# The first half's output projection as seven products, and attention chunks loaded from ScalarE's queue

## The chip, the cores and the metric

The kernel runs on one core of a Trainium2 chip. The metric is the time of one execution on the device, in microseconds (us). The time before is a median of three runs. One further execution was profiled, and all views of the profile come from that one.

## The reference

One layer of a hybrid decoder block, on 2048 tokens of width 1024, in float32. The cut to what matters here:

```python
h = rmsnorm(x, norm1_g)
q, k, v, g, a, c_b, c_c, c_h = split(h @ w_in)            # gate a: rank 16
log_a = log_sigmoid(a @ w_gate_up + b_gate) / 16
o = gla_chunked(q / 8, k, v, log_a)                       # 4 heads, 64 x 128; state runs over the tokens
o_gla = rmsnorm(o, gla_norm_g) * silu(g)                  # width 512
o_conv = c_b * causal_depthwise_conv(c_c * c_h, conv_w)   # width 512, 3 taps
x = x + concat([o_gla, o_conv]) @ w_out                   # the output projection, 1024 x 1024
h2 = rmsnorm(x, norm2_g)
x = x + (silu(h2 @ w_ffn_gate) * (h2 @ w_ffn_up)) @ w_ffn_down
return rmsnorm(x, norm_f_g)
```

## The kernel before, in words

The 2048 tokens are four blocks (b) of 512, two to a half. All work is written in one function, and a scheduler of the framework, which simulates the engines, places each instruction; the order on every engine is then fixed in the program, and semaphores order the engines among one another.

**Products in float32.** Each operand is split into a high and a low part: ScalarE rounds (L146), VectorE subtracts (L147). A step of a product is then three matmuls, 128 x 128 by 128 x 512, lines L328 to L330: high by high, high by low, low by high.

**Two forms of a projection.** `unit` multiplies a 2 x 2 arrangement of quarters, two blocks of output columns by the two token blocks of a half, in seven products instead of eight (Strassen's scheme): seven products of four steps of three matmuls, 84 in all. It takes sums of weight quarters, which `unit_weights` makes on the way (seven splits, four combinations on GpSimd at L311 to L318), and operands in seven forms: the token operand's quarters B11, B21, B22 and the combinations T1 to T4. After a product `copied` takes a bank to SBUF on ScalarE (L348), and `plus` adds a bank on VectorE (L352). The plain form, in `out_proj`, needs eight products and only the operand's quarters: a half's output projection is 384 matmuls (L722, L723, L725) with 16 operand pairs, which `build_mix` loads as split values, from `s_gla` (attention) and `s_mix` (convolution).

**The sequence.** `in_proj(0)`, `in_proj(1)` (12 units each), `out_proj(0)`, `out_proj(1)`, then the feed-forward part in two halves. `in_proj(1)` begins with 28 operand pairs loaded from `s_h1` (`siB`, `siT` in the profile), which were made beside `in_proj(0)`. The operand pool holds 28 pairs, so loads of a next stage wait for products of the last.

**Attention in the background.** `gla_half` is a generator that treats a half's eight chunks of 128 tokens: `gla_load` (14 transfers of 64 KB on SyncE's queue, then the decay factors, L609 to L612), `gla_scores` (L617 to L638), `gla_outputs` (L641 to about L690) and `gla_finish` (transposes L682, gating L683, a split and two stores to `s_gla`). `tick`, called after each product, advances the background on every second product, and a second generator list, `ahead`, on every fourth. The gate's decays are made by another background generator, `gate`, during in_proj. Buffers of attention come from the pool `bx` (11, tag "b"), most others from `tp` (9, tag "t").

`in_proj` stores q, k, v and g of each block to scratch in DRAM (`s_kq`, `s_v`, `s_g`; the gate's `s_d`), one tile to 128 rows, and at its end the convolution's values, split, to `s_mix`.

Of the kernel before, what the change touches and what calls it, by code (L numbers as in the profile page):

```python
# [47 lines left out]
def tile_hymba_block(ctx, tc, x, xt, win, wa, wgu, wout, wffn, wdown, wdown_first, small, out):  # L48
# [50 lines left out]
            [dram.tile([P, PB], F32, name=f"{name}{b}_{i}") for i in range(n)] for b in range(NB)  # L99
        ]  # L100

    s_kq, s_d, s_v, s_g = scratch("sk", 4), scratch("sd", 2), scratch("sv", 4), scratch("sg", 4)
    s_x1 = scratch("sx", KD)
    s_mix = [[dram.tile([P, 2, PB], F32, name=f"sm{b}_{k}") for k in range(4)] for b in range(NB)]
    s_gla = [dram.tile([P, HEADS, 2, PB], F32, name=f"sgla{b}") for b in range(NB)]
    s_act = [
        [
# [17 lines left out]
    def col(c):  # L125
        return sml[:, c : c + 1]
# [13 lines left out]
    def store(dst, src):  # L140
        return nc.sync.dma_start(dst, src)
# [32 lines left out]


    background = []
    pace, ahead, hurry = [0], [], []

    def step():
        while background:  # L180
# [6 lines left out]
    def tick():  # L187
        pace[0] += 1
        if pace[0] % 2 == 0 or hurry:
            step()  # L190
        elif ahead and pace[0] % 4 == 1:
            next(ahead[0], None)

    def unhurried():
# [95 lines left out]
        return ops, [(r, j, o[r, j], True) for j in range(2) for r in range(2)]  # L290

    def weight_quarter(src):
        n = src.shape[-1]
        h = wqp.tile([P, 2, PB], F32R, name="wq", tag="wq")[:, :, 0:n]
        split(src, h[:, 0, :], h[:, 1, :])
        return h

    def raw_weights(src):
# [3 lines left out]
        raw_loads.append(load(raw, src))  # L302
        return raw

    def unit_weights(src):
        raw = raw_weights(src)
        n = src.shape[-1]
        a11, a12, a22, a21 = [raw[:, i, :] for i in range(4)]
        s1 = rawp.tile([P, PB], F32, name="s1", tag="s1", bufs=1)[:, 0:n]
        w = {"A11": weight_quarter(a11)}  # L310
        pool.tensor_tensor(s1, a21, a22, ALU.add)  # L311
        pool.tensor_tensor(a21, a11, a21, ALU.subtract)  # L312
        pool.tensor_tensor(a11, s1, a11, ALU.subtract)  # L313
# [4 lines left out]
        pool.tensor_tensor(a12, a12, a11, ALU.subtract)  # L318
        w["S4"] = weight_quarter(a12)
        w["A22"] = weight_quarter(a22)  # L320
        return w
# [7 lines left out]
        pe.matmul(o[:], wh, xl, start=False, stop=False, skip_group_check=True)  # L329
        return pe.matmul(o[:], wl, xh, start=False, stop=k == n - 1, skip_group_check=True)  # L330

    def unit(src, ops, into=None):


        w = unit_weights(src)
# [171 lines left out]
    def forget_gate(b, a_sb):  # L507
# [3 lines left out]
        for i in range(2):  # L511
# [20 lines left out]
            store(s_d[b][i][:], t2[:])  # L532
            yield
        decays[b] = em, dn, el

    def in_proj(half, ops, first):
# [7 lines left out]
        units = units()  # L544
        for dst, i0 in ((s_kq, 0), (s_kq, 2), (s_v, 0), (s_v, 2)):
            for r, j, c, p in next(units):
                store(dst[2 * half + j][i0 + r][:], settled(c, p)[:])
        for i0 in (0, 2):
            for r, j, c, p in next(units):
                store(s_g[2 * half + j][i0 + r][:], silu(c, p)[:])  # L550
        background.append(gla_half(half))
        for i0 in (0, 2):
            cc = {(r, j): settled(c, p) for r, j, c, p in next(units)}
# [14 lines left out]
            for r, j, c, _ in next(units):  # L568
                y = cc[r, j]
                dve.tensor_tensor(y[:], c[:], y[:], ALU.mult)  # L570
                hi = tp.tile([P, PB], F32R, name="hi", tag="t")
                split(y[:], hi[:], y[:].bitcast(F32R))
                dst = s_mix[2 * half + j][i0 + r]
                store(dst[:, 0, :], hi[:].bitcast(F32))
                store(dst[:, 1, :], y[:])


    def gla_half(half):
        chunks = [(b, t) for b in (2 * half, 2 * half + 1) for t in range(PT)]
        with tc.issue_after(last_silu[0].ins):  # L580
            tables = act.preload_act_table_set("natural_log_exp_and_others")
        with tc.issue_after(tables.ins):
            nxt = gla_load(*chunks[0])
        o = None
        for n, (b, t) in enumerate(chunks):
            cur = nxt
            s = gla_scores(b, t, *cur)
            yield
            if o is not None:
                gla_finish(*chunks[n - 1], *o)  # L590
                yield
            if n + 1 < len(chunks):
                nxt = gla_load(*chunks[n + 1])
            o = gla_outputs(b, t, *s)
            yield
        gla_finish(b, t, *o)
        done.add((b, t))
        yield
# [4 lines left out]
    def gla_load(b, t):  # L603
        s = slice(t * P, (t + 1) * P)
        kq, e, vt, g = [bt(n, (P, 4, P)) for n in ("kq", "ee", "vt", "gt")]
        for dst, src in ((kq, s_kq[b]), (e[:, 2:4, :], s_d[b]), (vt, s_v[b]), (g, s_g[b])):
            for i, r in enumerate(src):
                load(dst[:, i, :], r[:, s])
        act.activation(e[:, 0:2, :], e[:, 2:4, :], AF.Exp, scale=-1.0 / 16.0)  # L609
# [5 lines left out]
        return kq, e, vt, g  # L615
# [62 lines left out]
    def gla_finish(b, t, osb, g):  # L678

        ot = ps.tile([P, HEADS, P], F32, name="ot", tag="mm")  # L680
        for h in range(HEADS):
            pe.transpose(ot[:, h, :], osb[:, h, :], ident[:])  # L682
# [418 lines left out]
```

## Time and profile before

| what | value |
|---|---|
| time, median of 3 runs | 2146.97 us (2140.72 to 2151.3) |
| profiled execution: its time, its span | 2146.09 us, 2144.2 us |
| TensorE busy, share of span | 2043.6 us, 95% |
| VectorE, ScalarE, GpSimd busy | 68%, 47%, 46% |
| moved by DMA | 467.64 MB, mean 218 GB/s |
| in_proj(1), about 315 to 628 us: TensorE busy | 306.20 of 313 us |
| out_proj(0), about 628 to 727 us: TensorE busy | 98.65 of 99 us |

In the views a matmul group has the line, the engine, the tile names (out<-in), the shape and the count, and after the bar the busy time and the mean of one in ns, then the idle time in front of it and what released it. TensorE's matmuls overlap, so that the mean of one is not the distance between two. In the views by window a row has the stretch and its length, the busy time of PE (TensorE matmuls), PEld (its weight loads), DVE (VectorE), ACT (ScalarE) and POOL (GpSimd) with the number of instructions, then TensorE's granted clock, the DMA engines' share and their rate. SP is SyncE, which issues DMAs. A timeline row begins with the start and the duration in us, and ends with the idle time before it in brackets.

### The profile page before, as it was taken

To read this page: it belongs to the slowest core of one execution; us is meant where nothing else is said; L and a number is where in the kernel's file an instruction comes from. 1 tells how busy PE (TensorE), PEld (TensorE's weight loads), DVE (VectorE), ACT (ScalarE), POOL (GpSimd) and SP (SyncE) were. 2 spreads that over 40 slices of the span, in tenths; PEclk is the share of its full clock that TensorE was granted. 3 is DMA by queue.
4 is the path that set the end of the run, shared out by engine and by line. 5 is a ranking of instruction groups with operands and counts; after the bars stand their busy time and mean duration, and the time that the engine had idled before them with its cause. 6 is when DMAs were issued, how large, how long until landed. Compare 5 with 4: busy or idle time off the path is not lost.

```text
span 2144.2 us, 26906 instructions
## 1 busy us (share of the span) xinstructions
PE 2043.6 (95%) x9133; PEld 1651.3 (77%) x9133; DVE 1452.5 (68%) x2034; ACT 1012.1 (47%) x1962; POOL 997.0 (46%) x714
## 2 busy tenths in 40 slices
PE   4899899999999999999999999999999999999996
PEld 2677687887888887788888887787888888887775
DVE  8849965556774486888887664554686677664554
ACT  4555434574544235555454553333454454553344
POOL 4526422122201274655655436774644654445774
PEclk9999999999999999999999999999999999999998
DMA  4259658532577884465464577689455455487662
GB/s 150 76 199 315 218 228 286 156 125 79 166 247 256 309 294 152 167 240 220 172 237 182 185 303 283 254 336 355 157 191 205 154 197 196 172 329 293 266 265 108
DMA packets 189977, 467.64 MB, mean 218 GB/s; under 512 B 19856, under 2 KB 65168, under 8 KB 180112
## 3 DMA queue, kind: packets, MB, share of 16 engines
q1 hardware_dynamic: 189840, 465.93, 59.9%
q8 instruction: 72, 1.18, 0.2%
q14 instruction: 65, 0.53, 0.1%
HBM read 297.03 MB, written 168.82 MB: 217 GB/s over the span
## 4 chain that ended last, share of the span: by engine, by line
PE 70%; DVE 11%; DMA 8%; issue 4%; ACT 3%; POOL 3%; SPq 1%; DVEq 0%; POOLq 0%; ACTq 0%
PE mm L328 20%; PE mm L330 20%; PE mm L329 19%; DVE wq L147 3%; PE mm L722 3%; PE mm L725 3%; PE mm L723 3%; DMA raw<-in_wdown_dram 2%; DVE h L440 2%; DMA raw<-in_wffn_dram 1%; DVE so L147 1%; DVE op L147 1%; DMA op<-shT 1%; DVE c L352 1%; ACT wq L146 1%
## 5 line engine op out<-in xcount | busy, mean ns | idle before, releaser
L328 PE MATMUL mm<-op,wq 128*128 128x512 f32 x2495 | 982.1, 395 | 33.0 <-ACT c L348 20.3
L330 PE MATMUL mm<-op,wq 128*128 128x512 f32 x2495 | 967.6, 392 | 12.4 <-DVE wq L147 11.2
L329 PE MATMUL mm<-op,wq 128*128 128x512 f32 x2495 | 975.6, 391 | 2.5 <-DVE op L147 2.5
L147 DVE TENSOR_TENSOR wq<-raw,wq 128x512 fp32r<-128x512 f32 (+2 forms) x628 | 536.6, 860 | 320.2 <-ACT wq L146 318.3
L146 ACT ACTIVATE wq<-raw 128x512 fp32r<-128x512 f32 (+2 forms) x628 | 367.1, 589 | 566.7 <-PE mm L330 415.4
L328 PEld LDWEIGHTS mm<-op,wq 128*128 128x128 f32 x2495 | 470.4, 189 | 152.1 <-ACT c L348 27.1
L330 PEld LDWEIGHTS mm<-op,wq 128*128 128x128 f32 x2495 | 470.5, 189 | 121.9 <-DVE wq L147 22.4
L329 PEld LDWEIGHTS mm<-op,wq 128*128 128x128 f32 x2495 | 470.7, 189 | 99.8 <-DVE op L147 3.0
L313 POOL TENSOR_TENSOR raw<-s,raw 128x512 f32<-128x512 f32 (+2 forms) x98 | 130.7, 1333 | 437.7 <-DVE wq L147 403.1
L352 DVE TENSOR_TENSOR c<-mm,c 128x512 f32<-128x512 f32 x270 | 185.1, 686 | 100.1 <-PE mm L330 98.0
L311 POOL TENSOR_TENSOR s<-raw 128x512 f32<-128x512 f32 (+2 forms) x98 | 130.8, 1335 | 207.9 <-DMA raw<-in_wffn_dram 96.1
L318 POOL TENSOR_TENSOR raw<-raw 128x512 f32<-128x512 f32 (+2 forms) x98 | 130.4, 1331 | 129.5 <-DVE wq L147 128.9
L348 ACT ACTIVATE c<-mm 128x512 f32<-128x512 f32 x270 | 156.4, 585 | 23.8 <-PE mm L330 23.0
L704 POOL TENSOR_TENSOR ssx<-ssx,q 128x512 f32<-128x512 f32 x52 | 75.2, 1459 | 151.0 <-ACT q L703 151.0
L312 POOL TENSOR_TENSOR raw<-raw 128x512 f32<-128x512 f32 (+2 forms) x98 | 137.2, 1400 | 4.6
L884 POOL TENSOR_TENSOR y<-c,y 128x512 f32<-128x512 f32 x66 | 98.6, 1496 | 67.3 <-DVE c L352 67.2
L147 DVE TENSOR_TENSOR so<-t,so 128x512 fp32r<-128x512 f32 x100 | 89.6, 902 | 23.8 <-ACT so L146 23.6
L722 PE MATMUL mm<-op,wq 128*128 128x512 f32 x256 | 100.9, 394 | 0.0
L723 PE MATMUL mm<-op,wq 128*128 128x512 f32 x256 | 99.7, 390 | 0.0
L146 ACT ACTIVATE wq<-s 128x512 fp32r<-128x512 f32 (+2 forms) x98 | 57.6, 588 | 89.2 <-PE mm L330 86.6
L147 DVE TENSOR_TENSOR wq<-s,wq 128x512 fp32r<-128x512 f32 (+2 forms) x98 | 81.9, 835 | 15.6 <-ACT wq L146 15.2
L146 ACT ACTIVATE so<-t 128x512 fp32r<-128x512 f32 x100 | 62.9, 630 | 48.6 <-DMA sa_B<-so 19.9
(177 smaller groups left out, 1931.2 us busy)
## 6 DMA issues: line engine op xcount, KB each, us to landing
raw<-in_wffn_dram SPq DMA_DIRECT2D x44, 1024.0 KB, 6.1
sa_T<-so SPq DMA_DIRECT2D x88, 512.0 KB, 4.9
op<-sa_T SPq DMA_DIRECT2D x88, 512.0 KB, 9.6
sa_B<-so SPq DMA_DIRECT2D x69, 512.0 KB, 3.4
op<-sa_B SPq DMA_DIRECT2D x69, 512.0 KB, 9.2
raw<-in_win_dram SPq DMA_DIRECT2D x24, 1024.0 KB, 5.7
raw<-in_wdown_dram SPq DMA_DIRECT2D x24, 768.0 KB, 6.1
sx<-y SPq DMA_DIRECT2D x48, 256.0 KB, 3.4
```

What stands on the lines that cost most here:

```text
L146: last_hi[:] = [act.activation(hi, src, AF.Copy)]
L147: return dve.tensor_tensor(lo, src, hi.bitcast(F32), ALU.subtract)
L311: pool.tensor_tensor(s1, a21, a22, ALU.add)
L312: pool.tensor_tensor(a21, a11, a21, ALU.subtract)
L313: pool.tensor_tensor(a11, s1, a11, ALU.subtract)
L328: pe.matmul(o[:], wh, xh, start=first and k == 0, stop=False, skip_group_check=True)
L329: pe.matmul(o[:], wh, xl, start=False, stop=False, skip_group_check=True)
L330: return pe.matmul(o[:], wl, xh, start=False, stop=k == n - 1, skip_group_check=True)
L348: act.activation(t[:], o[:], AF.Copy)
L352: dve.tensor_tensor(t[:], o[:], t[:], ALU.add)
L722: pe.matmul(o[e, j][:], wh, m[:, 0, :], start=k == 0, stop=False)
L723: pe.matmul(o[e, j][:], wh, m[:, 1, :], start=False, stop=False)
```

## The change

- The scratch tiles `s_kq`, `s_d`, `s_v`, `s_g` become one tile to a block. `gla_load` is now four transfers (`ee` 128 KB, `kq`, `vt`, `gt` 256 KB each) issued by ScalarE instead of 14 issued by SyncE, and in `gla_half` it stands ahead of `gla_finish` instead of behind it. The decays move to a function of their own, `gla_decay`, called after `gla_outputs`. `done` is now told of every chunk, and not only of a half's last one.
- For the first half, the attention's and the convolution's values are stored unsplit, to `s_val`. A generator `mix_ahead`, in the list `ahead`, loads them during in_proj(1), makes the seven forms of operands (16 subtractions on GpSimd, 28 splits) and stores them to `s_mixp`. B21, B22 and B11 come as their values are there; T1 to T4 in twelve steps after chunk (1,3), the last of the first half. With the list `often` filled, `ahead` advances on every odd product.
- `out_first` takes the place of `out_proj(0)`: four calls of `unit` with `mixed=True` (which rearranges the output weights' layout in SBUF to quarters), that is 4 x 84 = 336 matmuls, with 28 operand pairs loaded from `s_mixp`. `out_proj(1)` stays as it is.

```diff
-    s_kq, s_d, s_v, s_g = scratch("sk", 4), scratch("sd", 2), scratch("sv", 4), scratch("sg", 4)
+    s_kq, s_d = gathered("sk", 4), gathered("sd", 2)
+    s_v, s_g = gathered("sv", 4), gathered("sg", 4)
...
+    s_val = [
+        [dram.tile([P, PB], F32, name=f"sw{b}_{k}") for k in range(KD)] for b in range(2)
+    ]
+    s_mixp = {
+        n: [dram.tile([P, 2, PB], F32, name=f"sy{n}_{k}") for k in range(4)] for _, n in PRODUCTS
+    }
...
-        elif ahead and pace[0] % 4 == 1:
+        elif ahead and (pace[0] % 4 == 1 or often):
             next(ahead[0], None)
...
-    def unit_weights(src):
+    def unit_weights(src, mixed=False):
...
+        if mixed:
+            tiles = raw.rearrange("p a n -> p (a n)").rearrange("p (i k e c) -> p i k e c", i=2, k=4, e=2)
+            a11, a12, a21, a22 = [tiles[:, i, :, e, :] for e in range(2) for i in range(2)]
+            s1 = s1.rearrange("p (k c) -> p k c", c=P)
...
                 dve.tensor_tensor(y[:], c[:], y[:], ALU.mult)
+                if half == 0:
+                    store(s_val[j][4 + i0 + r][:], y[:])
+                    continue
                 hi = tp.tile([P, PB], F32R, name="hi", tag="t")
...
             s = gla_scores(b, t, *cur)
             yield
+            if n + 1 < len(chunks):
+                nxt = gla_load(*chunks[n + 1])
             if o is not None:
                 gla_finish(*chunks[n - 1], *o)
+                done.add(chunks[n - 1])
                 yield
+            o = gla_outputs(b, t, *s)
             if n + 1 < len(chunks):
-                nxt = gla_load(*chunks[n + 1])
-            o = gla_outputs(b, t, *s)
+                gla_decay(*nxt)
             yield
...
-        for dst, src in ((kq, s_kq[b]), (e[:, 2:4, :], s_d[b]), (vt, s_v[b]), (g, s_g[b])):
-            for i, r in enumerate(src):
-                load(dst[:, i, :], r[:, s])
+        for dst, src in ((e[:, 2:4, :], s_d[b]), (kq, s_kq[b]), (vt, s_v[b]), (g, s_g[b])):
+            act.dma_start(dst[:], src[:, :, s])
+        return kq, e, vt, g
+
+    def gla_decay(kq, e, vt, g):
         act.activation(e[:, 0:2, :], e[:, 2:4, :], AF.Exp, scale=-1.0 / 16.0)
...
+        if b < 2:
+            for h in range(HEADS):
+                store(s_val[b][h][:, t * P : (t + 1) * P], osb[:, h, :])
+            return
         split(osb[:], g[:].bitcast(F32R), osb[:].bitcast(F32R))
...
+    def mix_ahead():
+        def put(n, k, h):
+            hi, lo = [bx[0].tile([P, PB], F32R, name=e, tag="b") for e in ("hi", "lo")]
+            split(h[:], hi[:], lo[:])
+            for e, y in enumerate((hi, lo)):
+                store(s_mixp[n][k][:, e, :], y[:].bitcast(F32))
+
+        def fetch(j, k):
+            h = bt("h")
+            load(h[:], s_val[j][k][:])
+            return h
+
+        for n, j, k0 in (("B21", 0, 4), ("B22", 1, 4), ("B11", 0, 0)):
+            while n == "B11" and (0, PT - 1) not in done:
+                yield
+            h = fetch(j, k0)
+            yield
+            for k in range(4):
+                cur = h
+                if k < 3:
+                    h = fetch(j, k0 + k + 1)
+                put(n, k, cur)
+                yield
+        while (1, PT - 1) not in done:
+            yield
+        b11, b12 = fetch(0, 0), fetch(1, 0)
+        yield
+        for k in range(4):
+            b22, t1 = fetch(1, 4 + k), bt("t1")
+            pool.tensor_tensor(t1[:], b12[:], b11[:], ALU.subtract)
+            put("T1", k, t1)
+            yield
+            b21 = fetch(0, 4 + k)
+            pool.tensor_tensor(t1[:], b22[:], t1[:], ALU.subtract)
+            put("T2", k, t1)
+            pool.tensor_tensor(b12[:], b22[:], b12[:], ALU.subtract)
+            put("T3", k, b12)
+            yield
+            if k < 3:
+                b11, b12 = fetch(0, k + 1), fetch(1, k + 1)
+            pool.tensor_tensor(t1[:], b21[:], t1[:], ALU.subtract)
+            put("T4", k, t1)
+            yield
...
+    def out_first(ops):
+        ssq = [tiny.tile([P, PB], F32, name=f"ssx{j}", tag=f"ssx{j}", bufs=1) for j in range(2)]
+        begun = set()
+        for d0 in range(0, KD, 2):
+            ys = {}
+            for e in range(2):
+                for j in range(2):
+                    ys[e, j] = tt("y")
+                    load(ys[e, j][:], xt[j, :, d0 + e, :])
+            for e, j, c, p in unit(wout[d0 // 2], ops, mixed=True):
+                y = ys[e, j]
+                (dve if p else pool).tensor_tensor(y[:], y[:], c[:], ALU.add)
+                store(s_x1[j][d0 + e][:], y[:])
+                sum_squares(ssq[j], y[:], j not in begun)
+                begun.add(j)
+        return ssq
...
     background.append(gate(1, ops))
+    ahead.append(mix_ahead())
+    often.append(True)
     in_proj(1, ops, None)
     drain_background(lambda: (1, PT - 1) in done)
-    ssq = out_proj(0, build_mix(0))
+    for _ in ahead.pop():
+        pass
+    often.clear()
+    ssq = out_first(load_pairs(s_mixp))
```

More of the change, by code (lines that the diff above doesn't have):

```diff
@@ L100, in scratch, with gathered @@
         ]
-    s_kq, s_d, s_v, s_g = scratch("sk", 4), scratch("sd", 2), scratch("sv", 4), scratch("sg", 4)
+    def gathered(name, n):
+        return [dram.tile([P, n, PB], F32, name=f"{name}{b}") for b in range(NB)]
+    s_kq, s_d = gathered("sk", 4), gathered("sd", 2)
+    s_v, s_g = gathered("sv", 4), gathered("sg", 4)
     s_x1 = scratch("sx", KD)
     s_mix = [[dram.tile([P, 2, PB], F32, name=f"sm{b}_{k}") for k in range(4)] for b in range(NB)]
+    s_val = [
[4 more added lines that the diff above has]
+    }
     s_gla = [dram.tile([P, HEADS, 2, PB], F32, name=f"sgla{b}") for b in range(NB)]
@@ L176, in tile_hymba_block @@
     background = []
-    pace, ahead, hurry = [0], [], []
+    pace, ahead, hurry, often = [0], [], [], []
     def step():
@@ L292, in weight_quarter @@
     def weight_quarter(src):
-        n = src.shape[-1]
+        n = src.shape[-1] if len(src.shape) == 2 else PB
         h = wqp.tile([P, 2, PB], F32R, name="wq", tag="wq")[:, :, 0:n]
-        split(src, h[:, 0, :], h[:, 1, :])
+        hi, lo = h[:, 0, :], h[:, 1, :]
+        if len(src.shape) == 3:
+            hi, lo = [y.rearrange("p (k c) -> p k c", c=P) for y in (hi, lo)]
+        split(src, hi, lo)
         return h
@@ L330, in product_step, with unit @@
         return pe.matmul(o[:], wl, xh, start=False, stop=k == n - 1, skip_group_check=True)
-    def unit(src, ops, into=None):
-        w = unit_weights(src)
+    def unit(src, ops, into=None, mixed=False):
+        w = unit_weights(src, mixed)
         def mul(i, o=None):
@@ L531, in forget_gate @@
             dve.tensor_tensor(dn[:, i, :], em[:, i, :], el[:, i, :], ALU.mult)
-            store(s_d[b][i][:], t2[:])
+            store(s_d[b][:, i, :], t2[:])
             yield
@@ L546, in in_proj @@
             for r, j, c, p in next(units):
-                store(dst[2 * half + j][i0 + r][:], settled(c, p)[:])
+                store(dst[2 * half + j][:, i0 + r, :], settled(c, p)[:])
         for i0 in (0, 2):
             for r, j, c, p in next(units):
-                store(s_g[2 * half + j][i0 + r][:], silu(c, p)[:])
+                store(s_g[2 * half + j][:, i0 + r, :], silu(c, p)[:])
         background.append(gla_half(half))
@@ L588, in gla_half @@
             yield
+            if n + 1 < len(chunks):
+                nxt = gla_load(*chunks[n + 1])
             if o is not None:
                 gla_finish(*chunks[n - 1], *o)
+                done.add(chunks[n - 1])
                 yield
+            o = gla_outputs(b, t, *s)
             if n + 1 < len(chunks):
-                nxt = gla_load(*chunks[n + 1])
-            o = gla_outputs(b, t, *s)
+                gla_decay(*nxt)
             yield
@@ L614, in gla_load @@
         )
-        return kq, e, vt, g
     def gla_scores(b, t, kq, kt, v, g):
```

## The prediction

> **What bounds the kernel now.** I read the page's share table and chain first, then the windows around the places that the change touches, then the DMA, timeline and group views inside those windows.
>
> ```profile
> span 2144.2 us, 26906 instructions
> PE 2043.6 (95%) x9133; PEld 1651.3 (77%) x9133; DVE 1452.5 (68%) x2034; ACT 1012.1 (47%) x1962; POOL 997.0 (46%) x714
> PE 70%; DVE 11%; DMA 8%; issue 4%; ACT 3%; POOL 3%; SPq 1%; DVEq 0%; POOLq 0%; ACTq 0%
> L722 PE MATMUL mm<-op,wq 128*128 128x512 f32 x256 | 100.9, 394 | 0.0
> ```
>
> TensorE is busy for 95% of the span and carries 70% of the chain, so time is won by removing matmuls or TensorE's pauses, and lost by a new pause. The mean of 394 ns in the last row is not the price of a matmul, because neighbours overlap. The price is the distance between starts, in TensorE's timeline:
>
> ```profile
> 339.01 0.39 PE L329 MATMUL mm<-op,wq 128*128 128x512 f32 x1
> ...
> 343.32 0.39 PE L330 MATMUL mm<-op,wq 128*128 128x512 f32 x1
> 347.42 1.23 PE L622 MATMUL sc<-kq 64*128 64x128 f32 x8 [3.72 <-issue]
> ...
> 350.35 0.63 PE L329 MATMUL mm<-op,wq 128*128 128x512 f32 x1
> 350.77 0.63 PE L330 MATMUL mm<-op,wq 128*128 128x512 f32 x1
> ...
> 354.03 0.40 PE L329 MATMUL mm<-op,wq 128*128 128x512 f32 x1
> ```
>
> From 339.01 to 343.32 lie 19 steps, 0.227 us each. The same rows show the only long pause that bears on this change, at the start of in_proj(1): 3.72 us without work, and behind it a step of 0.42 us (350.35 to 350.77) until about 354.0. So 6.6 us (347.4 to 354.0) ran at half speed, which loses another 3.3 us. The Trainium skill (TensorE: Matmul & The Clock Gate, Part 1: The HAM clock gate) has TensorE fall to half clock after an idle window of about 3.4 us, for about as long; the idle row agrees, while the half speed lasted 6.6 us: by the page's length the loss would be 1.7 us, an estimate, where the trace has 3.3.
>
> What surrounds that pause is the model for the new out_proj(0), so its windows and transfers matter most (columns: stretch and length, busy PE, PEld, DVE, ACT, POOL, granted clock, DMA share, GB/s):
>
> ```profile
> 310.00:320.00 10.00, 10.00 (x54) 7.91 (x53) 8.90 (x15) 6.65 (x19) 1.67 (x1) 1.00 1.03 412
> 330.00:340.00 10.00, 10.00 (x58) 8.38 (x58) 4.72 (x15) 5.62 (x18) 1.29 (x1) 1.00 1.03 406
> 605.00:645.00 40.00, 40.00 (x214) 32.94 (x213) 27.19 (x59) 18.41 (x48) 1.29 (x1) 1.00 0.89 310
> 645.00:720.00 75.00, 74.65 (x379) 61.67 (x379) 29.40 (x63) 27.87 (x73) 13.88 (x10) 1.00 0.76 257
> ```
> ```profile
> 295.15 1.01 SPq L138 DMA_DIRECT2D op<-siB  x2
> ...
> 333.86 0.32 SPq L138 DMA_DIRECT2D kq<-sk  x1
> 334.57 0.32 SPq L138 DMA_DIRECT2D op<-siT  x1
> ```
> ```profile
> DMA packets 7806, 19.02 MB, mean 366 GB/s; under 512 B 800, under 2 KB 3067, under 8 KB 7675
> ...
> op<-siT SPq DMA_DIRECT2D x16, 512.0 KB, 7.7
> op<-siB SPq DMA_DIRECT2D x12, 512.0 KB, 8.8
> ```
>
> in_proj(1) loads 28 operand pairs of 512 KB, beginning when the products of in_proj(0) release them. The DMA engines are full then (share 1.03, 412 GB/s). The last operand is issued at 334.57 and lands 7.7 us later: 47 us in all. TensorE has 48 us of other work until 343.3, and still pauses, since the first chunk's values stand behind the operands on SP's queue. out_proj(0) now needs only 16 pairs, and has no pause (last two windows).
>
> **Part by part.** *Fewer matmuls.* out_proj(0) falls from 384 to 4 units of 84, that is 336: 48 x 0.227 = 10.9 us less. That is about 0.5% of the time, 10.7 us, which is about what a measurement of this kernel can tell from no change. All of these lie on TensorE in a stretch where it never waits (74.65 of 75 us), so the gain is real unless the new operands are late.
>
> *The new operands at out_proj(0).* They are now 28 loads of 512 KB, and must again wait for in_proj(1) to release their buffers. The groups of TensorE between 295.4 and 343.4, for the price of attention work:
>
> ```profile
> L328 PE MATMUL mm<-op,wq 128*128 128x512 f32 x58 | 23.3, 402 | 0.0
> L329 PE MATMUL mm<-op,wq 128*128 128x512 f32 x59 | 23.0, 390 | 0.0
> L330 PE MATMUL mm<-op,wq 128*128 128x512 f32 x59 | 22.7, 391 | 0.0
> L646 PE MATMUL o_ps<-vt,scores 128*128 128x128 f32 x16 | 2.6, 275 | 0.0
> ...
> L682 PE MATMUL ot<-ident,osb 128*128 128x128 f32 x4 | 0.6, 272 | 0.0
> ```
>
> There 176 large matmuls fill 39.9 us of 48.0, so the small ones cost 8.1 us for 72 (seven rows from L646 to L682, of which I show the ends), 0.113 us each. A whole chunk has 42: 4.7 us. In the built order of the changed kernel TensorE has, between the first release and the third product of the new first unit, 117 large matmuls (26.5 us) and two chunks (9.4 us): 36 us of cover, against 48 before in_proj(1). The queue ahead of the last operand holds 28 x 0.524 = 14.7 MB of operands, and 3.8 MB of weights, chunk values and the second half's convolution stores that stand between them: 18.5 MB, which at 0.41 MB a microsecond (the 412 and 406 GB/s above) take 45 us.
>
> That alone need not stop TensorE, because the products use the operands in the order of loading: the last group is wanted four products (4 x 12 x 0.227 = 10.9 us) after the 36 us, at 47 us. What stops it is the moved issue. The chunk loads now stand in ScalarE's own instruction order, and each carries a wait for the transfer eight places earlier over both queues. Ahead of the copy of c11, which the third product needs, stand the loads of chunks (3,1) and (3,2). Of these, ee of (3,1) waits for a store at 16.8 MB (41 us), and holds ScalarE's copy of vt that chunk (3,0)'s products need; vt of (3,2) waits for an s_gla store that itself waits for the last operand, at 20.4 MB: 49.8 us. Behind it on ScalarE are the squares, the copy of c11 and the weight splits, and for these waits TensorE. So I expect a pause of 49.8 - 36 = 14 us, perhaps in two pieces, and half speed behind it, 3.3 us by the timeline rows: +17.3. Bounds: nothing at all, if ScalarE is not held (47 us against 45); and 26, if the queue drains at the 366 GB/s that the whole window of the DMA view had (20.4 MB in 55.7 us, a pause of 19.7) and half speed follows two pieces (6.6). The upper half has the better ground, since the order of ScalarE is written in the program and the share of 1.03 was measured.
>
> *Making the operands.* The nearest rows between 280 and 830 us, where the groups show busy time and mean ns:
>
> ```profile
> L147 DVE TENSOR_TENSOR wq<-raw,wq 128x512 fp32r<-128x512 f32 x118 | 94.9, 808 | 89.6 <-ACT wq L146 89.5
> L146 ACT ACTIVATE wq<-raw 128x512 fp32r<-128x512 f32 x119 | 74.5, 627 | 113.8 <-PE mm L330 72.3 <-PE mm L725 28.2 <-POOL raw L318 5.5
> L249 POOL TENSOR_TENSOR t<-h,t 128x512 f32<-128x512 f32 x4 | 6.7, 1674 | 2.5 <-DVE op L147 2.5
> L609 ACT ACTIVATE ee<-ee 128x256 f32<-128x256 f32 x14 | 5.8, 414 | 17.2 <-DMA ee<-sd 17.2
> ```
> ```profile
> 520.00:540.00 20.00, 16.92 (x83) 12.58 (x83) 19.94 (x42) 8.42 (x19) 4.75 (x3) 1.00 0.36 105
> 540.00:560.00 20.00, 20.00 (x110) 16.52 (x107) 18.79 (x35) 12.90 (x33) 4.23 (x4) 1.00 0.55 176
> ```
>
> mix_ahead adds 28 splits (28 x 0.808 = 22.6 us of VectorE, 28 x 0.627 = 17.6 of ScalarE), 16 subtractions (x 1.674 = 26.8 us of GpSimd), and 84 transfers of 256 KB, 22 MB. 16 splits go away (8 of gla_finish, 8 of the convolution), but only the former from the same stretch. Spread over in_proj(1)'s 313 us this has room by the shares of the page (68, 47 and 46%), except at the gate: at 520 to 560 VectorE is full (19.94 and 18.79 of 20) and TensorE loses 3.1 us. About 7 of the new splits fall there by the built order, 5.7 us of VectorE; before, 20 us of full VectorE let through 3.1 us of pause. I take +2.5, between 0 and 5.7. The unit form of out_proj(0) has 28 weight splits for 16 and 16 combinations on GpSimd; in out_proj(0) VectorE is busy for 29.4 of 75 us and GpSimd for 13.9, which hides them; without that cover 12 x 0.8 = 10 us. I take +1, for the end of the last unit.
>
> *Chunk loads.* 14 transfers become 4, issued one chunk step earlier, and the 17.2 us that ScalarE waits at L609 may go, for which I count nothing, as ScalarE has 3% of the chain. At in_proj(1)'s start gt's load waits for a store 14.4 MB into the queue (14.4 / 0.41 = 35 us), before TensorE arrives at it, 39 us by the same count of the built order; of today's 3.72 + 3.3 us I let 2 go (between 7 gone and 3 more). The 8 x 4 chunk transfers beside in_proj(1) cost ScalarE issue time: 0.32 us each by the kq row is 10 us, four times that (four rows each) 41 us, in 313 us of an engine that is half idle (ACT 47%): nothing.
>
> Sum: -10.9 + 17.3 + 2.5 + 1 - 2 = +7.9 on the profiled run's 2146.1 us, 1.9 of them outside the span; that run lies 0.9 below the median of 2146.97, and I do not add this. **Forecast 2154 us.**
>
> **The rivals.** *A, hidden after all (2134):* the cover of 47 us against 45 holds because ScalarE's waits are met in time. For it: today's copies run ahead of need (645 to 720 without a pause), and DMA rows land 8 us after issue. Then what is left is -10.9 - 2 + 1 = -11.9, with the gate hidden too: 2134. With the whole pause at 343 gone it is 2129, with the gate's 2.5 paid 2137. The point of decision is whether a chunk load on ScalarE waits for an operand of out_first. The Trainium skill (DMA: Bandwidth & Descriptors, Issuing engines are not separate DMA queues) says that issuing from another engine saves only sequencer time, since all run on the same 16 engines. By it the move is worth little and costs nothing, which is this rival; the full DMA share at 310 to 340 agrees about the engines, and no row of before shows what a wait on ScalarE's queue costs.
>
> *B, ScalarE held at in_proj(1)'s start as well (slower, 2166):* there too the loads of two chunks stand on ScalarE before copies that TensorE needs, and 28 operands fill the queue. If gt's load, or the next chunk's, is held for over 3.4 us beyond TensorE's arrival, a second pause with its half speed (3.7 + 3.3 = 7) comes instead of the 2 us won, and the two pieces at out_first each bring half speed (3.3 more): 7.9 + 9 + 3.3 = +20. With out_first's pause at its bound of 19.7 it is +26, 2172. It decides from the point at which gt's load lands later than TensorE comes to it, 39 us after the first operand. Against it: gt's transfer stands at 35 us, and at the gate, the next place with chunk loads, the DMA share is 0.36 and 0.55.
>
> *C, the change does not do what it says:* the 48 matmuls could go and out_proj(0) be bound by DMA instead. But after its first unit nothing is loaded but weights and x, and 257 GB/s is far from 412. I give it no chance of its own.
>
> **How the numbers follow.** Forecast 0.47, with its own range 2146 to 2163 (the gate's 0 to 5.7, and the pause from 8, with one piece hidden, to 19.7); A 0.28; B 0.25. The range goes from A's 2132 to B's 2172, leaving out some 0.1 at each end. The bounds of no change are 2136.2 and 2157.7, 0.5% around the median: of A 0.18 lies below and 0.10 inside, of the forecast 0.33 inside and 0.14 above, and B is above. Faster 0.18, within 0.5% 0.43, slower 0.39.
>
> **What would show it.** In the profile after: 4 units of 84 matmuls at a step of 0.227 us in out_proj(0); a pause of TensorE about 36 us after the first new operand load, released by ScalarE (a copy of vt or c11) while ScalarE itself is idle behind a chunk load; 40 to 50 us of DMA share 1.0 there; a pause at the gate of 3 to 9 us. No pause before the first unit would make the forecast wrong towards A, and pauses of over 3.4 us at both halves' starts towards B.

## The result, and the profile after

The changed kernel takes 2183.72 us (median of 4 runs, 2180.51 to 2186.02) against 2143.84 us before (4 runs, the three of the section on the time before and a fourth of 2140.24 taken beside the changed kernel): a ratio of 1.0173, 95% interval 1.0155 to 1.0192. It is slower by about 40 us, outside the predicted range. The profiled execution has a span of 2184.3 us against 2144.2.

First the page: the span, the engines' shares and the chain by engine.

```profile
span 2184.3 us, 26912 instructions
PE 2050.2 (94%) x9085; PEld 1653.3 (76%) x9085; DVE 1486.9 (68%) x2058; ACT 1027.4 (47%) x1998; POOL 1061.1 (49%) x758
PE 72%; DVE 11%; DMA 9%; issue 3%; ACT 3%; POOL 1%; ACTq 0%; SPq 0%; DVEq 0%; POOLq 0%
```

48 matmuls are gone (9133 to 9085), and yet TensorE is busy for 6.6 us longer: a first sign that some of them ran at half speed. The shares hide the rest, because 40 us are 2% of the span. The windows at out_proj(0)'s start do not hide it (columns as before: busy PE, PEld, DVE, ACT, POOL, granted clock, DMA share, GB/s):

```profile
630.00:640.00 10.00, 10.00 (x60) 8.37 (x58) 4.46 (x10) 1.77 (x4) 0.00 (x0) 1.00 1.05 400
640.00:650.00 10.00, 6.98 (x24) 5.38 (x23) 10.00 (x21) 6.89 (x21) 1.27 (x1) 0.83 1.00 359
650.00:660.00 10.00, 7.83 (x44) 5.88 (x42) 5.05 (x10) 1.40 (x4) 3.85 (x3) 1.00 1.02 338
660.00:670.00 10.00, 0.00 (x0) 0.00 (x0) 0.00 (x0) 0.00 (x0) 0.00 (x0) 0.53 1.03 413
670.00:680.00 10.00, 4.15 (x24) 3.79 (x24) 3.63 (x11) 5.91 (x19) 0.00 (x0) 0.67 1.08 388
680.00:690.00 10.00, 8.12 (x23) 6.44 (x24) 2.72 (x6) 3.45 (x7) 1.89 (x2) 0.60 0.57 176
```

From 660 to 670 us no engine computes at all, while the DMA engines are full. TensorE's timeline has three pauses there, with the releaser in brackets, and the chain of waits says what ScalarE in turn had waited for (total, times, longest):

```profile
643.25 0.51 PE L346 MATMUL mm<-op,wq 128*128 128x512 f32 x1 [3.02 <-DVE c L370]
...
671.12 0.80 PE L672 MATMUL o_ps<-vt,scores 128*128 128x128 f32 x2 [13.29 <-ACT vt L659]
...
681.88 0.79 PE L346 MATMUL mm<-op,wq 128*128 128x512 f32 x1 [6.61 <-ACT c L366]
```
```profile
ACT ee L658 <- DMA sm<-hi: 18.8, 1, 18.8
...
ACT wq L157 <- DMA op<-syT: 8.1, 1, 8.1
```

ScalarE's own timeline has the order of these instructions (ACTq is an issue of a transfer by ScalarE):

```profile
650.81 0.62 ACT L157 ACTIVATE wq<-raw 128x512 fp32r<-128x512 f32 x1
669.62 0.53 ACTq L632 DMA_DIRECT2D ee<-sd  x1
670.19 0.39 ACT L658 ACTIVATE ee<-kt_ps 128x256 f32<-128x256 f32 x1 [18.77 <-DMA sm<-hi]
670.47 0.59 ACT L659 ACTIVATE vt<-v_ps 128x512 f32<-128x512 f32 x1
```

The order to read them: o_ps (L672) needs vt; vt's copy on ScalarE (L659) stands behind L658 in ScalarE's order, and in front of both stands the issue of the next chunk's `ee`, which by the releaser waits for a store of convolution values (`sm<-hi`) that is queued among the operands. In the same way the 8.1 us ends with an issue (of `gt`, at 638.10) that waits for an operand (`syT`) to land. Neither instruction reads what it waits for. In the third pause ScalarE no longer stands behind a load for long: from 675.9 to 681.2 it does the squares and carries that had been held, issues the next three transfers, and only then copies c11. (The chunk at 671 us is (3,1) and the next (3,2): the prediction numbers them one too low.) The operands' own issues on SyncE's queue:

```profile
619.85 2.37 SPq L149 DMA_DIRECT2D op<-syB  x4
...
664.25 0.32 SPq L149 DMA_DIRECT2D op<-syT  x1
```

The rest is seen by placing both executions beside each other at five marks that each kernel has: the first operand load of in_proj(1), the first score matmul (`sc<-kq`) of chunk 7 and of chunk 11 (counted from 0), and the first row-sum matmul (`tot<-ssx`) of the first and of the second half's second norm. I call the last one the FFN mark; it lies after out_proj(1) and within the first unit of the feed-forward part. Before they stand at 295.1, 454.9, 589.2, 740.0 and 847.8 us, after at 295.1, 459.5, 603.6, 774.6 and 887.0. So the change costs 4.6 us at in_proj(1)'s start, 9.9 between chunks 7 and 11, where the gate is, and 24.8 (20.1 of them up to the first half's mark) from chunk 11 to the FFN mark, where 48 matmuls, 10.9 us, have gone. All that lies behind the FFN mark adds 0.8.

### The profile page after: what moved, and what is told of

Read it like the earlier page. It is cut to its first block, busy times and chain, and to the rows that moved or that the text cites. A ratio compares the mean times of both kernels' runs of the same rounds, so it can differ in the third digit from the quotient of the medians.

```text
span 2184.3 us, 26912 instructions
## 1 busy us (share of the span) xinstructions
PE 2050.2 (94%) x9085; PEld 1653.3 (76%) x9085; DVE 1486.9 (68%) x2058; ACT 1027.4 (47%) x1998; POOL 1061.1 (49%) x758
## 4 chain that ended last, share of the span: by engine, by line
PE 72%; DVE 11%; DMA 9%; issue 3%; ACT 3%; POOL 1%; ACTq 0%; SPq 0%; DVEq 0%; POOLq 0%
PE mm L346 21%; PE mm L348 21%; PE mm L347 21%; DVE wq L158 2%; DMA raw<-in_wdown_dram 2%; DVE h L458 1%; PE mm L816 1%; PE mm L817 1%; PE mm L819 1%; DMA op<-sa_B 1%; DMA op<-siT 1%; DVE lo L158 1%; DVE so L158 1%; DMA op<-shT 1%; DVE op L158 1%
## 5 line engine op out<-in xcount | busy, mean ns | idle before, releaser
L346 PE MATMUL mm<-op,wq 128*128 128x512 f32 x2607 | 1032.3, 398 | 43.7 <-ACT c L366 26.9
L348 PE MATMUL mm<-op,wq 128*128 128x512 f32 x2607 | 1016.1, 394 | 14.8 <-DVE wq L158 14.0
L347 PE MATMUL mm<-op,wq 128*128 128x512 f32 x2607 | 1024.7, 393 | 2.5 <-DVE op L158 2.5
L158 DVE TENSOR_TENSOR wq<-raw,wq 128x512 fp32r<-128x512 f32 (+2 forms) x636 | 544.0, 862 | 328.8 <-ACT wq L157 325.5
L346 PEld LDWEIGHTS mm<-op,wq 128*128 128x128 f32 x2607 | 494.5, 190 | 168.7 <-ACT c L366 33.2
L348 PEld LDWEIGHTS mm<-op,wq 128*128 128x128 f32 x2607 | 495.0, 190 | 131.2 <-DVE wq L158 26.2
L347 PEld LDWEIGHTS mm<-op,wq 128*128 128x128 f32 x2607 | 495.1, 190 | 104.7 <-DVE op L158 3.0
L331 POOL TENSOR_TENSOR raw<-s,raw 128x512 f32<-128x512 f32 (+2 forms) x102 | 136.2, 1335 | 439.0 <-DVE wq L158 432.7
L370 DVE TENSOR_TENSOR c<-mm,c 128x512 f32<-128x512 f32 x282 | 193.0, 685 | 109.0 <-PE mm L348 106.1
L329 POOL TENSOR_TENSOR s<-raw 128x512 f32<-128x512 f32 (+2 forms) x102 | 135.5, 1328 | 185.5 <-DMA raw<-in_wffn_dram 92.5
L336 POOL TENSOR_TENSOR raw<-raw 128x512 f32<-128x512 f32 (+2 forms) x102 | 137.1, 1344 | 138.6 <-DVE wq L158 137.3
L366 ACT ACTIVATE c<-mm 128x512 f32<-128x512 f32 x282 | 163.1, 586 | 46.3 <-PE mm L348 41.8
L330 POOL TENSOR_TENSOR raw<-raw 128x512 f32<-128x512 f32 (+2 forms) x102 | 142.8, 1400 | 4.9
L158 DVE TENSOR_TENSOR so<-t,so 128x512 fp32r<-128x512 f32 x100 | 90.2, 908 | 22.9 <-ACT so L157 22.6
L916 DVE TENSOR_TENSOR c<-c,c 128x512 f32<-128x512 f32 x66 | 67.7, 1026 | 0.1
L920 POOL TENSOR_TENSOR t<-c,c 128x512 f32<-128x512 f32 x44 | 61.7, 1402 | 5.6 <-DVE c L916 5.6
```

The costliest lines, as they stand in the source:

```text
L158: return dve.tensor_tensor(lo, src, hi.bitcast(F32), ALU.subtract)
L346: pe.matmul(o[:], wh, xh, start=first and k == 0, stop=False, skip_group_check=True)
```

## The experiments

All times in the table are of the profiled executions, minus the kernel before, by stage; the ratio is that of the timed runs. Differences behind the FFN mark, where no experiment changes anything, run from -3.8 to +7.0 us, and those ahead of the first mark from -6.0 to +0.9, so that a total of one profile is good to a few us, and the three stages are the better witness.

| kernel | in_proj(1)'s start | gate, chunks 7 to 11 | chunk 11 to FFN mark | ratio to before, 95% interval |
|---|---|---|---|---|
| changed | +4.6 | +9.9 | +24.8 | 1.0173 (1.0155 to 1.0192) |
| e1_sp | -5.0 | +8.5 | +9.4 | 1.0067 (1.0044 to 1.0089) |
| e1_pool | -4.2 | +10.6 | +14.5 | 1.0114 (1.0093 to 1.0135) |
| e2_loads | +3.1 | +3.8 | +5.2 | 1.0073 (1.0052 to 1.0095) |
| e6_loads_sp | -6.0 | +0.1 | +1.4 | 0.998 (0.9965 to 0.9996) |
| e3_first | +3.2 | +12.2 | +19.7 | 1.016 (1.0138 to 1.0182) |
| e4_gate | -5.0 | +7.8 | +22.2 | 1.0119 (1.0092 to 1.0146) |
| e5_store | -5.0 | +9.6 | +12.0 | 1.0092 (1.0069 to 1.0114) |
| e7_both | -5.0 | +10.2 | +19.2 | 1.0124 (1.0094 to 1.0155) |
| e8_few | +4.9 | +10.4 | +1.8 | 1.0051 (1.0036 to 1.0067) |
| e9_few_not | +4.1 | +3.7 | +1.3 | 1.0031 (1.0018 to 1.0043) |
| e10_few_not_sp | -4.9 | +0.1 | -3.8 | 0.9933 (0.9912 to 0.9955) |

**Who issues the chunk loads: e1_sp, e1_pool.** The edit, in `gla_load` (e1_pool has `pool.dma_start`):

```diff
-            act.dma_start(dst[:], src[:, :, s])
+            load(dst[:], src[:, :, s])        # SyncE
```

> The changed kernel, with the four chunk transfers of each chunk issued by SyncE instead of ScalarE, at the same places. Held-issue theory: ScalarE is no longer held at out_first (in the changed kernel three pauses of 3.0, 13.3 and 6.6 us and half speed after each, some 30 us) nor at in_proj(1)'s start (4.1 us and half speed), so 22 to 34 us come back: 2150 to 2162, and no pause of TensorE over 4 us at out_first. Full-queue theory (the transfers are late because 20 MB stand ahead of them, whoever issues them): 2175 to 2190, and TensorE waits at out_first for operands or chunk values instead.

> The changed kernel, with the chunk transfers issued by GpSimd. Held-issue theory: the wait holds GpSimd instead, which makes the sums of weight quarters for out_first's first unit; the sums are needed later than the copy of c11, so most but not all comes back: 2150 to 2172, with GpSimd idle for over 5 us at the same place. Full-queue theory: 2175 to 2190.

Measured: 2162.67 and 2172.41 us. With SyncE as issuer 21 us come back (the expectation's upper end was 2162), by the profiles 9.6 at in_proj(1)'s start and 15.4 behind chunk 11. That ScalarE was held by its issues is shown for these. But a pause of 12.32 us stays at out_first, against the expected 4:

```profile
657.86 0.79 PE L346 MATMUL mm<-op,wq 128*128 128x512 f32 x1 [12.32 <-ACT c L366]
```
```profile
ACT c L366 <- DMA sm<-hi: 8.6, 1, 8.6
```

ScalarE waits here to write the copy of c11: its buffer (pool `tp`) still holds convolution values whose store stands among the operands on SyncE's queue. GpSimd as issuer gives 16.7 us at the same copy, and its total lies between the ranges of the two theories, so it tells little.

**The loads alone: e2_loads, e6_loads_sp.** The kernel before with gathered scratch and the four transfers at the earlier place, `out_proj(0)` unchanged; e6_loads_sp differs from e2_loads by the edit above alone.

> The kernel before with the chunk loads alone changed (gathered scratch, four transfers on ScalarE's queue, the earlier place, the decays on their own); out_proj(0) keeps its plain product. Held-issue theory: only in_proj(1)'s start is hit (+4.6 us at the first chunk after it, as the changed kernel has), since out_proj(0) loads 16 pairs and not 28: 2143 to 2153 against 2144. If ScalarE's queue costs in itself: 2160 or more.

> The kernel of e2_loads (out_proj(0) as before), with the four chunk transfers on SyncE. e1_sp won 5.7 us at in_proj(1)'s start against the kernel before; if gathered and earlier loads are what won it, this has it too, without any loss later: 2138 to 2146 where the kernel before has 2144 to 2149. Rival (the gain came from the operands no longer being split at the end of in_proj(0)): within 3 us of before.

Measured: 2163.63 and 2142.23 us, before 2149.42 and 2147.46 beside them. The same transfers, called for at the same places of the program, cost about 20 us more from ScalarE than from SyncE (0.9% by the ratios; 16.6 us by the three stages of the profiles). e2_loads is 10 us above what I expected and where the other case of its expectation has it: ScalarE's queue costs in itself. ScalarE loses at other places than in_proj(1)'s start too (+3.8 at the gate, +5.2 behind chunk 11, where only 16 pairs are loaded). Below are its largest pause, and the stretch around it in the kernel before and in e6_loads_sp (TensorE busy for 16.28 and for 19.39 of 20 us; in e2_loads it is 13.86, at a granted clock of 0.83 and a DMA share of 1.01). Between 295 and 345 us ScalarE of e2_loads once waits 13.1 us for an operand of SyncE's queue (`op<-siB`), and in e6_loads_sp never:

```profile
336.14 0.80 PE L332 MATMUL mm<-op,wq 128*128 128x512 f32 x1 [7.60 <-ACT c L352]
```
```profile
330.00:350.00 20.00, 16.28 (x88) 13.50 (x88) 9.97 (x22) 8.48 (x24) 2.60 (x2) 0.93 0.92 309
```
```profile
330.00:350.00 20.00, 19.39 (x107) 15.96 (x106) 9.54 (x22) 10.20 (x27) 2.59 (x2) 1.00 1.06 368
```

The pause of 3.72 us that the kernel before had at in_proj(1)'s start is gone in e6_loads_sp, and the two later stages lose 1.5 us by its profile: of the versions that compute what the reference does it is the only one faster than the kernel before, by 0.2%, with an interval that ends just below 1. Its stage there wins 6.0 us (e1_sp, by the same marks, 5.0 and not the 5.7 of the expectation). Which part wins it, fewer transfers, their order or the earlier place, was not separated.

**The seven products alone: e3_first.** `gla_load` and `gla_half` as before (14 transfers of SyncE, the later place), the rest as changed.

> The changed kernel with the chunk loads as before (14 transfers of SyncE, the old place); out_first and mix_ahead stay. Held-issue theory: in_proj(1)'s start as before, the gate's loss stays (10 us in the changed kernel), out_first costs at most a pause of 4 us with half speed like in_proj(1)'s start, and 48 matmuls are saved: 2140 to 2156. Full-queue theory: 2170 or more.

Measured: 2182.19 us. My expectation was wrong by 26 us at least. Without any issue on ScalarE the loss is about the same, so ScalarE's queue is one way of losing it, and not the only one. TensorE's largest pause at out_first is now at the chunk values, 6.74 us at chunk 14, whose loads stand behind the operands on SyncE's queue, as they did at in_proj(1)'s start before; another of 4.69 us is at a copy of ScalarE. At in_proj(1)'s start and at the gate the first chunk's values come 7.08 and 6.65 us late:

```profile
683.52 1.22 PE L643 MATMUL sc<-kq 64*128 64x128 f32 x8 [6.74 <-DVE kq L633]
```

**Moving the new waits: e5_store, e4_gate, e7_both,** all upon e1_sp. e5_store issues the second half's convolution stores from GpSimd; e4_gate holds T1 to T4 back until the gate is done; e7_both has both.

```diff
-                store(dst[:, 0, :], hi[:].bitcast(F32))
-                store(dst[:, 1, :], y[:])
+                pool.dma_start(dst[:, 0, :], hi[:].bitcast(F32))
+                pool.dma_start(dst[:, 1, :], y[:])
...
-        while (1, PT - 1) not in done:
+        while (1, PT - 1) not in done or 3 not in decays:
             yield
```

> The kernel of e1_sp, with the stores of the second half's convolution values issued by GpSimd instead of SyncE. Buffer theory (the copy of c11 waits for a buffer whose store stands among the operand loads on SyncE's queue, a pause of 12.3 us): the pause falls under 5 us and half speed goes with it, 9 to 14 us less than e1_sp: 2148 to 2154. Rival (the operands themselves are late): the pause stays, now on an operand, 2160 or more.

> The kernel of e1_sp (chunk loads on SyncE), with T1 to T4 of mix_ahead held back until the gate of the second half is done. Collision theory (16 splits and 16 subtractions fall on the stretch where VectorE is full): the loss between chunks 7 and 11, 8.5 us in e1_sp against the kernel before, falls to 1 to 4 us: 4 to 8 us less than e1_sp, 2154 to 2159. Rival (VectorE's total is the matter, wherever it lies): within 3 us of e1_sp, 2160 to 2166.

> The edits of e4_gate and e5_store together. If both theories hold and are independent, 14 to 22 us less than e1_sp: 2141 to 2149, about the time of the kernel before. If T1 to T4, now later, run into the operand loads, 2152 or more.

Measured: 2165.81, 2173.06 and 2174.33 us, so none was faster than e1_sp: e5_store is in the range of its rival, e4_gate lies above both of its ranges, and e7_both is in its second case. In e5_store the pause at c11 fell to 3.59 us, as the buffer theory said, and a pause of 7.80 us came 17 us later, at chunk values that now stand behind the operands:

```profile
649.78 0.50 PE L346 MATMUL mm<-op,wq 128*128 128x512 f32 x1 [3.59 <-ACT c L366]
...
666.58 1.23 PE L648 MATMUL sc<-kq 64*128 64x128 f32 x8 [7.80 <-DVE kq L639]
```

A wait was replaced by its neighbour. In e4_gate the gate itself is relieved (counted from chunk 7, chunk 8 comes 9.2 us earlier than in the kernel before, in e1_sp 2.7), but by chunk 11 the loss is back at 7.8, and the stage behind it is worse by 13 us, with a pause at chunk 13:

```profile
643.93 1.23 PE L648 MATMUL sc<-kq 64*128 64x128 f32 x8 [8.80 <-DVE kq L639]
```

The work of T1 to T4 has no free place between the gate and out_first in these two tries. A full VectorE is not the whole of it: from 540 to 600 us of e4_gate TensorE stands idle for 7.65 us while VectorE is busy for 18.24, 13.68 and 14.94 of 20 us, and ScalarE waits 18 us between 510 and 600 for the subtractions and the stores of T1 to T4. The profiled executions of e4_gate and e7_both (spans 2164.6 and 2164.2) are the fastest of their runs; much of that lies outside the table's stages (e4_gate is 6.0 us ahead at the first mark, e7_both wins 3.8 behind the last).

**Less to load: e8_few, e9_few_not, e10_few_not_sp.** e8_few loads 12 pairs and uses B11, B21 and B22 in the places of T1 to T4, e9_few_not does not make T1 to T4 either, e10_few_not_sp has besides the chunk loads on SyncE.

```diff
-    ssq = out_first(load_pairs(s_mixp))
+    few = {n: [load_pair(p) for p in s_mixp[n]] for n in ("B11", "B21", "B22")}
+    few.update(T1=few["B11"], T2=few["B11"], T3=few["B21"], T4=few["B22"])
+    ssq = out_first(few)
...
-        while (1, PT - 1) not in done:      # e9, e10
-            yield
+        return
```

> The changed kernel, but out_first loads only the 12 pairs of B11, B21 and B22 and uses them in the places of T1 to T4 as well (T1 to T4 are still made and stored, so out_first computes something else). Queue theory (the three pauses at out_first come from 8.4 MB more of operands ahead of the transfers for which ScalarE and the buffers wait): what was due at 16.8 to 20.4 MB comes at 8.4 to 12 MB, 20 to 29 us, inside the cover of 36 us; the 22.9 us of pauses and their half speed go: 2148 to 2158. Rival (a load on ScalarE's queue, or seven products instead of eight, costs this in itself): 2170 or more.

> As e8_few, and T1 to T4 are not made at all (16 subtractions, 16 splits, 16 fetches and 32 stores less). Collision theory: the loss between chunks 7 and 11, 9.9 us in the changed kernel, falls to 0 to 4: 6 to 10 us less than e8_few, 2139 to 2151. Rival (the gate's loss comes from the chunk loads on ScalarE): within 3 us of e8_few.

> As e9_few_not, with the chunk loads on SyncE. What is left is 48 matmuls fewer (10.9 us), the gathered loads at in_proj(1)'s start (5.7 to 6 us won) and the splits of B11, B21, B22: 2128 to 2138 where before has 2144 to 2149. If the sum does not close (2142 or more), the seven products have a price of their own in out_first.

Measured: 2160.16, 2155.08 and 2134.45 us; the first two are 2 and 4 us above their ranges, the third is inside. e8_few, with ScalarE still issuing, has the loss behind chunk 11 down from 24.8 to 1.8 us. The windows from 640 to 700 us of the changed kernel and of e8_few:

```profile
640.00:700.00 60.00, 37.08 (x165) 29.58 (x165) 28.28 (x55) 21.64 (x58) 13.64 (x10) 0.77 0.81 287
```
```profile
640.00:700.00 60.00, 56.34 (x299) 45.23 (x298) 45.18 (x75) 32.23 (x85) 25.90 (x19) 0.97 0.70 227
```

So what makes the waits long is the loads of the operands, as the queue theory says; the issuer only decides which instruction stands behind them. (12 pairs are fewer bytes and also need fewer buffers back from in_proj(1); the two were not tried apart.) From e8_few to e9_few_not the gate's loss falls from 10.4 to 3.7 us, the size that e2_loads has there, so making T1 to T4 is worth 6 to 7 us of it. The rest goes where ScalarE's loads go: e10_few_not_sp, which differs by their issuer, has 0.1. The two costs do not simply add: with T1 to T4 made, taking the loads off ScalarE wins 1.4 us (e1_sp, 8.5), and without them 3.6. The windows around it, of the changed kernel and of e9_few_not (VectorE, the third column, falls from 20.00 and 19.47 to 17.56 and 16.91 of 20 us):

```profile
530.00:550.00 20.00, 15.26 (x73) 11.56 (x72) 20.00 (x33) 8.03 (x19) 9.74 (x6) 0.91 0.51 164
550.00:570.00 20.00, 16.89 (x85) 13.76 (x84) 19.47 (x38) 11.19 (x29) 8.34 (x5) 0.91 0.64 213
```
```profile
530.00:550.00 20.00, 15.80 (x78) 12.86 (x77) 17.56 (x40) 7.40 (x19) 2.98 (x3) 0.83 0.36 101
550.00:570.00 20.00, 20.00 (x112) 16.55 (x111) 16.91 (x28) 11.05 (x27) 7.65 (x4) 1.00 0.62 215
```

With all three costs away, e10_few_not_sp is 13 us faster than before by the medians. Its profiled execution is the slowest of its four and wins 6.8: 4.9 at in_proj(1)'s start and 3.8 behind chunk 11, where 48 matmuls should give 10.9, with small losses elsewhere. Two pauses at the feed-forward part's first unit take most of the 7.1 us between; before there was one, of 2.32 us, at 826:

```profile
810.93 0.50 PE L346 MATMUL mm<-op,wq 128*128 128x512 f32 x1 [1.97 <-ACT wq L157]
...
815.14 0.79 PE L348 MATMUL mm<-op,wq 128*128 128x512 f32 x1 [3.48 <-DVE wq L158]
```

From chunk 12 to the FFN mark TensorE is idle for 6.7 us against 2.7 in the kernel before, and half speed (steps of 0.43 us from 815.14 to 819.57) takes another 2.2; 0.9 us stay open. The changed kernel has the same pair, 1.96 and 3.11 us. In the ten kernels with seven products the pauses here come to between 2.18 and 6.58 us, in the three with eight to between 1.47 and 2.83. Why the first weights of the feed-forward part are split later there was not tried.

## Why the prediction was wrong, step by step

The forecast was +7.9 us, the profile shows +40.1. By the terms of the sum:

- **48 matmuls, -10.9, and +1 for the end of the last unit:** the matmuls are all gone, from a stretch in which TensorE had not waited. Right as a count; but about 6 of the 10.9 us were lost again between the first half's mark and the FFN mark, at the feed-forward part's first unit: idle time is 2.8 us more (1.96 and 3.11 us against 2.32), and half speed from 862.69 to 868.9 takes about 3. The sum had +1. That step failed: I looked for what hides the new work inside out_proj(0), and not for what is late behind it. That the shorter out_proj(0) makes it late is likely and not shown. The stretch between the two marks, before and after (clock 1.00 and 0.95):

```profile
740.00:848.00 108.00, 105.68 (x462) 86.46 (x461) 86.81 (x96) 48.07 (x83) 62.52 (x40) 1.00 0.65 230
```
```profile
774.60:887.00 112.40, 107.33 (x454) 87.04 (x453) 86.88 (x96) 48.12 (x83) 62.23 (x40) 0.95 0.68 237
```

- **The pause at out_first, +17.3 with bounds of 0 and 26:** the mechanism is as predicted for the largest pause, down to the instructions: vt's copy behind the issue of the next chunk's `ee`, ScalarE idle behind a transfer that it doesn't need. (That the wait is for the transfer eight places earlier no view shows; the releasers agree with it.) The cover was right too: TensorE ran out of work 38 us after the first operand load, 3 of them the first pause, and the sum had 36. The size is beyond its upper bound of 26. TensorE stood idle for 22.9 us instead of 14; from chunk 12 to the first half's mark the stretch is 20.1 us longer although some 42 matmuls (9.5 us, by the records) less lie in it and idle time is 22.6 more, which leaves about 7 us for half speed instead of 3.3: 29.6 against 17.3.

  Two factors were wrong. The queue did not drain at 410 GB/s: from 620 to 670 us the mean is 363 (306, then the 400, 359, 338 and 413 of the windows above), so the last operand was issued 44.4 us after the first, where the sum had it landed at 45, and `ee` was let go after 49.8 us and not after 41. (That 49.8 is also the sum's figure for the end of the second hold is chance.) With the 366 GB/s of the bound the sum has a pause of 19.7, and the last two pauses have 19.9 together.

  And there were three pieces, not one or two, each with half speed behind it. The first, 3.02 us, follows ScalarE's wait of 8.1 us for an operand at in_proj(1)'s end, which the sum did not have, and a VectorE that is full from 640 to 650 us; that the one leads to the other was not tried. The third is not a second hold but the work that the first one had piled up on ScalarE.
- **in_proj(1)'s start, -2:** it was +4.6, beyond the bound of 3 more. The prediction weighed only gt's load, and rival B's mechanism, ScalarE held there as well, is what happened (13.2 us behind `ee`, and PE's wait for vt's copy, below). That the gathered, earlier loads by themselves win 6 us there (e6_loads_sp) was in the bounds, but the change issued them from ScalarE, where it is lost.

```profile
337.01 0.79 PE L672 MATMUL o_ps<-vt,scores 128*128 128x128 f32 x2 [4.13 <-ACT vt L659]
...
351.39 0.72 PE L648 MATMUL sc<-kq 64*128 64x128 f32 x8 [1.77 <-issue]
```
```profile
ACT wq L157 <- DMA ee<-sd: 13.2, 1, 13.2
```

- **The gate, +2.5 with bounds of 0 and 5.7:** it was +9.9. Without T1 to T4 it is 6.7 less (e9_few_not against e8_few), and what is left, 3.7, comes from ScalarE's loads (e2_loads has 3.8, e10_few_not_sp 0.1). The first was bounded by the VectorE time of the splits that I counted into 520 to 560 us; that left out the half speed after the pauses (granted clock 0.91 in both windows of the changed kernel above) and the waits for T1 to T4 on ScalarE, which e4_gate shows where VectorE has room. The second the prediction put at nothing: it counted the chunk loads' issue time on ScalarE, and not what an issue may have to wait. Together the terms now come to -10.9 + 29.6 + 6 + 4.6 + 9.9, and 0.8 behind the FFN mark: 40.0.
- **Rivals.** A (hidden, 2134) did not happen. That e10_few_not_sp reaches 2134.45 is luck in part: A was worked out with 1 us of rest and 2 us won, the run's profile has 7 and 5, and it loads and makes less. B, 2166 to 2172, had the right mechanism, ScalarE held at both starts, and is 12 us short of 2183.72 at its upper end. It lacked most of the gate's loss, the third piece and the loss at the feed-forward part.
- **The rule of the Trainium skill** (DMA: Bandwidth & Descriptors, Issuing engines are not separate DMA queues), that issuing from another engine only saves sequencer time, holds for the engines themselves, which are full whoever issues (shares of 1.03 and 1.06 in the windows above). As a price it fails here: about 20 us lie between e2_loads and e6_loads_sp, which differ in the issuer alone, and in e2_loads an issue that must wait holds ScalarE's own work (13.1 us).

The chances were wrong in the same way: I put 0.39 on slower by over 0.5%, and gave the terms ranges one by one, while all but the matmuls' came out on the slow side, and two of them, the two starts, have one cause. The gate's range added a pause and not the half speed that can follow it.

## What to carry to other kernels

Before a stage is made cheaper in matmuls, count what it must load at its start against the work that TensorE has meanwhile: here 28 operand pairs instead of 16, with the chunk loads moved to ScalarE, turned a start almost without pauses into 23 us of idle time, for 11 us saved. Think twice before an engine that computes issues loads that may have to wait, as everything behind them in its order waits as well; here the same transfers from SyncE, which does no computing, won a little time against the kernel before. And where a queue is the cause, taking away the wait that ends last only shows the next one (e5_store, e4_gate): halve the bytes first, to see what the queue is worth.

## What the runs showed of the hardware that I had not expected

Each of the three pauses at out_first brought half speed, also the first of only 3.02 us, whose window from 640 to 650 us has a granted clock of 0.83 (the others' 0.53 to 0.67 and 0.60). The length of a pause alone does not tell whether it will: pauses of 1.92 us were followed by steps of 0.43 us (e6_loads_sp at 524.32 and e10_few_not_sp at 525.58, granted clock 0.66 from 525 to 530), and a pause of 1.88 us at 535 and one of 3.23 at 891 in the kernel before, and one of 3.59 in e5_store at 649.78, were not (1.00). Nor does half speed last equally long: 3.7 us after the pause at 643, 6.6 after the one at 347 in the kernel before. With the DMA share at 1.00 to 1.08 from 630 to 680 us, what was moved ranged from 338 to 413 GB/s from one window of 10 us to the next; the share alone doesn't tell the rate.
